# Strassen products in 23 instead of 20 of the down-projection's 44 weight pairs, five of them from sums made earlier

## The chip, the core and the metric

The kernel runs on one core of one Trainium2 chip. The metric is the device time of one launch in microseconds, all loads and stores included. The five engines have queues of their own: TensorE (PE) multiplies, VectorE (DVE) and ScalarE (ACT) work elementwise, GpSimd (POOL) helps with small things, and SyncE (SP) issues nearly all DMA transfers, one after the other in the order of the program.

## What is computed

The reference is one layer of a decoder for 256 tokens of width 2048: a mixing block (sparse attention beside a convolution module), then a gated MLP with a causal depthwise convolution of three taps, then a last RMSNorm. The change lies in the MLP, whose inner width is 5632:

```python
def conv_glu_ffn(h, w_up, cw, cb, w_down):
    u = causal_depthwise_conv(h @ w_up, cw, cb)
    a, gate = jnp.split(u, 2, axis=-1)
    return (jax.nn.silu(gate) * a) @ w_down
...
        h = rms_norm(x, ffn_norm_g[l])
        x = x + conv_glu_ffn(h, w_up[l], ffn_conv_w[l], ffn_conv_b[l], w_down[l])
    return rms_norm(x, final_norm_g)
```

All numbers are float32. The kernel writes each factor as a rounded high part and a low rest (both in the type fp32r) and adds three partial products: high by high, low by high and high by low.

## The kernel before

**Up-projection.** It has 22 groups, m = 0 to 21, and each group uses four weight chunks of 128 x 2048 numbers (1 MB): first the a half of the inner columns, then the gate half, each in two halves of the depth. A group gives 256 inner columns for all 256 tokens. Behind the matmuls a list of stages follows each half group, one stage per chunk: `join` and `three_taps` (bias and convolution), and after the gate half also `gate` (silu times a, the tile g32), `g_high` and `g_low` (the high part stays in the tile gh, the low part goes through the tile glt to DRAM, glf).

**Down-projection.** Its depth of 5632 is cut into 22 pairs of 2 x 128 rows, and its 2048 output columns into two halves, h = 0 and 1, so there are 44 weight pairs of 1 MB, used in the order h = 0, p = 0 to 21, then h = 1. A pair is a 2 x 2 block product: two token halves by two depth tiles by two column blocks of 512. A pair of kind D makes it in the plain way with 8 block products. A pair of kind S uses Strassen's method (Winograd's form) with 7 block products. For that it needs four sums of its weight blocks, made by DVE in `down_split` into the tile `sums` and split into the tiles xh and xl, and four sums of the activation blocks. The latter are made once per p in the up-projection by `g_sums` on POOL, split into gsht and gslt, stored to DRAM (gsf0h, gsf0l, ...) and loaded back as gsh and gsl two pairs ahead by `sum_load`. One block product is four matmuls in `mm_down` (lines 200 to 203): activation block high by weight high (512 columns), low by high (256 columns), high by low (512), low by high (the other 256). With S pairs at p = 4, 6, 8, 9, 11, 13, 14, 16, 18 and 19 in both halves there are 20 of kind S and 24 of kind D.

**Weight stream.** All chunks stand in one list. Three buffers (`wraw`) take the loads. `w_next` hands over the weights of the chunk that is due and calls `w_split` or `down_split` for chunks up to two ahead: ACT writes the high part, DVE the low part, and then `w_dma` emits the next load of the list. That load waits until its buffer, three chunks back, has been read. Every DMA of the stream, the stores of glt, gsht and gslt and the loads of gl (the low activations), gsh and gsl stand in SP's one queue in the order in which the program emits them.

**Where the two stages meet.** In `down_pair` for the first pair the remaining up-projection stages are flushed (with the last two stores of glt), the pool `fu` of the up-projection's working tiles is closed, and the pool `fd` is opened in its memory (`late_pool`: wh4, wl4 for every fourth pair, sums, gsh, gsl). Then come `sum_load`, `w_next` and the products:

```python
            run_todo(3)
            sum_load(22 * h + p + 2)
            ws = w_next()
...
            for name, gi, w in products(kind, j):
```

Of the kernel before, what the change touches and what calls it, by code (L numbers as in the profile page):

```python
# [17 lines left out]
P = 128  # L18
# [20 lines left out]
SPAIRS = (4, 6, 8, 9, 11, 13, 14, 16, 18, 19)  # L39
KINDS = ["".join("DS"[p in SPAIRS] for p in range(22))] * 2  # L40

# [10 lines left out]
def hybrid_trunk(ctx: ExitStack, tc: tile.TileContext, a: dict, out: bass.AP):  # L52
# [20 lines left out]
    for qr, g in OUT_ORDER:  # L73
        chunks.append((a["w_o"][qr, g], CW))
    for m in range(NFT // 2):
        for part in range(2):
            for kh in range(2):
                chunks.append((a["w_u"][m, part, kh], CW))
    for h in range(2):
        for k2 in range(NFT // 2):  # L80
            chunks.append((a["w_d"][h, k2], CW))

    down0 = len(chunks) - NFT
    kinds = {down0 + i: k for i, k in enumerate(KINDS[0] + KINDS[1])}
# [3 lines left out]
    late, lows, late_pool = [], [], []  # L88
# [18 lines left out]

    def down_split(c):

        for f in lows[:]:  # L110
            f()
        lows.clear()
        raw = raws.pop(c)
        if (c - down0) % 4 == 3:
# [5 lines left out]
        if kinds[c] == "D":  # L120
# [7 lines left out]
        b, x = [raw[:, i * 512:(i + 1) * 512] for i in range(4)], late_pool[0].tile([P, CW], F32, name="sums", bufs=1)  # L128
        raw_low = sub_split(h[:, :1536], l[:, :1536], raw[:, :1536])
        nc.vector.tensor_add(x[:, :1024].rearrange("p (a c) -> p a c", a=2),  # L130
                             raw[:, :1024].rearrange("p (a c) -> p a c", a=2), b[3][:, None].to_broadcast([P, 2, 512]))
        nc.vector.tensor_add(x[:, 1024:1536], x[:, :512], b[1])
        nc.vector.tensor_add(x[:, 1536:], x[:, 1024:1536], b[2])  # L133
        raw_low()
        w_dma()
        lows.append(sub_split(xh, xl, x))

    def w_split(cuts):
# [5 lines left out]
        if c in kinds:  # L144
            return down_split(c)
# [23 lines left out]
    def w_next(cuts=1, ahead=LA):  # L169
        c = st["use"]  # L170
        st["use"] += 1
        w_pump()
        if st["split"] >= len(chunks):
            for f in lows:
                f()
            lows.clear()
        while st["split"] <= min(c + ahead, len(chunks) - 1):
# [832 lines left out]
    with ExitStack() as fx:  # L1010
# [3 lines left out]
        fu = up_only.enter_context(tc.tile_pool(name="fu", bufs=2))  # L1014
        gh_all = fp.tile([P, NFT, 2, P], F32R, name="gh")
# [22 lines left out]
        def sum_load(u):  # L1038
            if u < len(PAIRS) and PAIRS[u] == "S":
# [120 lines left out]
        def down_pair(h, p, g, j, nb):  # L1160
# [12 lines left out]
            if kind == "S":  # L1173
# [68 lines left out]
        for h in range(2):  # L1242
            nb = dict(zip((2, 3, 4, 8, 1, 5, 6, 7), ring[4 * h:] + ring[:4 * h]))
            for q in range(NQ):
# [13 lines left out]
                for j in range(2):  # L1258
                    p = 2 * q + j
                    down_pair(h, p, g, j, nb)  # L1260
                    if KINDS[h].rfind("S") == p:
# [92 lines left out]
```

## Time and profile before

| what | value |
|---|---|
| median of 3 runs (range) | 1093.67 us (1093.57 to 1093.92) |
| the profiled execution | 1093.86 us, its span 1092.1 us |
| up-projection, first to last matmul start | 362.5 to 852.3 us |
| down-projection, first to last matmul start | 852.4 to 1083.6 us |
| busy, share of the span | PE 99%, weight loads 88%, DVE 78%, ACT 55%, POOL 19% |
| HBM traffic | 226.29 MB read, 13.13 MB written |

The span runs from the first to the last instruction of the profiled execution, and its own time is 1.8 us longer. Matmuls of 512 columns have durations of about 394 ns in the rows, but follow one another in less, since they overlap, so the pace is read from starts. The releaser in square brackets is what ended the idle time of an engine before an instruction. For a DMA row the time is that of its issue on SP's queue.

### The profile page before, as it was taken

How to read it: one execution, taken by the hardware profiler on the slowest of the kernel's cores; microseconds unless marked ns; L12 is line 12 of the kernel's file. 1: busy time of each engine (PE TensorE's matmuls, PEld its weight loads, DVE VectorE, ACT ScalarE, POOL GpSimd, SP SyncE). 2: the span in 40 equal slices, each digit the busy share in tenths (PEclk: the TensorE clock that was granted, in tenths of full speed). 3: DMA queues.
4: the chain of work that ended last, by engine and by line, in shares of the span. 5: the costliest groups of instructions: out<-in, count | busy, mean ns of one | idle time of the engine just before them, and what ended most of it. 6: DMA issues, size and time to landing. Idle time of an engine off the chain costs nothing.

```text
span 1092.1 us, 17198 instructions
## 1 busy us (share of the span) xinstructions
PE 1080.5 (99%) x6778; PEld 959.7 (88%) x6778; DVE 857.2 (78%) x1369; ACT 601.2 (55%) x873; POOL 204.6 (19%) x171
## 2 busy tenths in 40 slices
PE   9999999999999999999999999999999999999997
PEld 8999999987788888888888888888888888888886
DVE  6899985776456677778777877887777899898996
ACT  7544456778635555555555555555555655554553
POOL 0888856647100000000000000000000000000000
PEclk9999999999999999999999999999999999999998
DMA  9676526323464655656566656665567688858982
GB/s 363 242 264 238 184 92 232 117 79 113 167 229 167 224 189 197 211 200 222 203 223 230 221 198 208 231 213 198 218 228 281 232 310 313 338 223 305 324 306 78
DMA packets 48125, 240.54 MB, mean 220 GB/s; under 512 B 5627, under 2 KB 7947, under 8 KB 24364
## 3 DMA queue, kind: packets, MB, share of 16 engines
q1 hardware_dynamic: 44668, 232.89, 59.9%
q10 hardware_dynamic: 3376, 6.55, 1.7%
q8 instruction: 53, 0.87, 0.3%
q14 instruction: 28, 0.23, 0.1%
HBM read 226.29 MB, written 13.13 MB: 219 GB/s over the span
## 4 chain that ended last, share of the span: by engine, by line
PE 92%; DVE 3%; DMA 3%; ACT 1%; issue 1%; POOL 0%; DVEq 0%; POOLq 0%; ACTq 0%
PE bank L1134 30%; PE bank L1136 15%; PE bank L200 6%; PE bank L202 6%; PE bank L191 5%; PE bank L193 4%; PE bank L192 4%; PE bank L203 3%; PE bank L201 3%; PE bank L210 3%; PE bank L208 3%; PE bank L209 3%; DMA wraw<-in_w_t 1%; PE bank L880 1%; PE bank L860 1%; DVE wl L158 1%
## 5 line engine op out<-in xcount | busy, mean ns | idle before, releaser
L1134 PE MATMUL bank<-xt,wh 128*128 128x512 f32 x1408 | 488.6, 394 | 0.0
L153 ACT ACTIVATE wh<-wraw 128x1024 fp32r<-128x1024 f32 (+2 forms) x193 | 269.9, 1418 | 293.3 <-issue 136.3
L1136 PE MATMUL bank<-xt,wl 128*128 128x256 f32 x1408 | 390.0, 277 | 0.0
L158 DVE TENSOR_TENSOR wl<-wraw,wh 128x2048 fp32r<-128x2048 f32 (+1 forms) x139 | 260.4, 1880 | 113.6 <-ACT wh L153 113.4
L1134 PEld LDWEIGHTS bank<-xt,wh 128*128 128x128 f32 x1408 | 264.0, 188 | 61.3
L1136 PEld LDWEIGHTS bank<-xt,wl 128*128 128x128 f32 x1408 | 264.2, 188 | 0.0
L191 PE MATMUL bank<-xt,wh 128*128 128x256 f32 x512 | 146.7, 287 | 0.9 <-ACT wh L301 0.9
L193 PE MATMUL bank<-xt,wl 128*128 128x256 f32 x512 | 145.2, 284 | 0.1
L192 PE MATMUL bank<-xt,wh 128*128 128x256 f32 x512 | 144.9, 283 | 0.0
L158 POOL TENSOR_TENSOR wl<-wraw,wh 128x1024 fp32r<-128x1024 f32 (+1 forms) x54 | 121.2, 2282 | 31.1 <-ACT wh L153 31.1
L105 ACT ACTIVATE wh<-wraw 128x2048 fp32r<-128x2048 f32 (+1 forms) x44 | 75.5, 1717 | 49.8 <-DMA wraw<-in_w_d 40.4
L191 PEld LDWEIGHTS bank<-xt,wh 128*128 128x128 f32 x512 | 98.0, 191 | 2.6 <-ACT wh L301 1.3
L192 PEld LDWEIGHTS bank<-xt,wh 128*128 128x128 f32 x512 | 98.1, 192 | 0.5
L193 PEld LDWEIGHTS bank<-xt,wl 128*128 128x128 f32 x512 | 98.1, 192 | 0.5 <-DVE wl L158 0.3
L106 DVE TENSOR_TENSOR wl<-wraw,wh 128x2048 fp32r<-128x2048 f32 (+1 forms) x44 | 89.9, 2044 | 7.2 <-ACT wh L105 7.2
L444 DVE SCALAR_TENSOR_TENSOR bank<-us,cw,bank 128x256 f32<-128x256 f32 x232 | 93.8, 481 | 1.0 <-ACT bank L439 0.5
L1047 POOL TENSOR_TENSOR gs<-g 128x256 f32<-128x256 f32 x10 | 7.4, 738 | 437.5 <-DVE g L1086 437.5
L200 PE MATMUL bank<-wh,gh 128*128 128x512 f32 x215 | 84.4, 393 | 0.0
L202 PE MATMUL bank<-wl,gh 128*128 128x512 f32 x215 | 84.4, 393 | 0.0
L1074 DVE SCALAR_TENSOR_TENSOR yt<-u,vecs,yt 128x255 f32<-128x255 f32 (+1 forms) x176 | 81.0, 481 | 3.1
L237 POOL TENSOR_TENSOR rstd<-ms,half 128x1 f32<-128x1 f32 x4 | 2.2, 556 | 346.4 <-DVE ms L230 346.4
L105 ACT ACTIVATE xh<-sums 128x2048 fp32r<-128x2048 f32 x20 | 38.4, 1921 | 49.9 <-DVE sums L133 49.9
(246 smaller groups left out, 1682.8 us busy)
## 6 DMA issues: line engine op xcount, KB each, us to landing
wraw<-in_w_u SPq DMA_DIRECT2D x88, 1024.0 KB, 4.9
wraw<-in_w_d SPq DMA_DIRECT2D x44, 1024.0 KB, 6.8
wraw<-in_w_t SPq DMA_DIRECT2D x29, 1024.0 KB, 5.0
wraw<-in_w_o SPq DMA_DIRECT2D x16, 1024.0 KB, 4.9
gl<-glf SPq DMA_DIRECT2D x22, 512.0 KB, 4.0
glf<-glt SPq DMA_DIRECT2D x22, 256.0 KB, 2.1
wraw<-in_w_vg SPq DMA_DIRECT2D x4, 608.0 KB, 3.7
hb<-in_head SPq DMA_DIRECT2D x4, 512.0 KB, 9.1
```

Source lines behind the costliest of these rows:

```text
L105: nc.scalar.activation(hi, src, AF.Copy)
L106: return lambda: nc.vector.tensor_sub(lo, src, hi.bitcast(F32))
L153: nc.scalar.activation(h[:, sl], raw[:, sl], AF.Copy)
L158: (nc.gpsimd if pooled else nc.vector).tensor_sub(l[:, sl], raw[:, sl], h[:, sl].bitcast(F32))
L191: nc.tensor.matmul(ps, wh, xh, start=first, stop=False)
L192: nc.tensor.matmul(ps, wh, xl, start=False, stop=False)
L193: nc.tensor.matmul(ps, wl, xh, start=False, stop=last)
L200: nc.tensor.matmul(ps, xh, wh, start=first, stop=False)
L202: nc.tensor.matmul(ps, xh, wl, start=False, stop=False)
L444: nc.vector.scalar_tensor_tensor(y[:, j] if last else acc[0], us[:, j, k:k + T], cw[:, j, k:k + 1], acc[0], op0=OP.mult, op1=OP.add)
L1134: nc.tensor.matmul(bk[i], wh[:, k, sl], xt[kt // 4][:, kt % 4].rearrange("p a t -> p (a t)"), start=kt == 0, stop=False)
L1136: nc.tensor.matmul(bk[i][:, :T], wl[:, k, sl], xt_h[kt], start=False, stop=kt == KD - 1)
```

## The change

Three more of the 44 pairs become Strassen pairs: 11 in the first column half and 12 in the second. Five of the 23 are of a new kind P: (h, p) = (0, 2), (0, 11), (1, 2), (1, 4), (1, 12). For these the weight block sums are made during the up-projection. Their weight chunk is put into the list a first time (kind X) ahead of the groups m = 2, 5, 9, 12 and 16. When its turn comes, `early_sums` makes the sums in the tile `early`, and the next `w_next` stores them to DRAM (sumf0 to sumf4). In the down-projection a P pair takes two entries of the list: the weights again, and behind them the sums from DRAM (kind T), which are then split without additions. The set of p that need activation sums is the union over both halves and grows from 10 to 15. Each column half keeps S pairs at p = 18 and 19, so the two stretches of work behind the last Strassen pair of a half stay as they are.

```diff
-SPAIRS = (4, 6, 8, 9, 11, 13, 14, 16, 18, 19)
-KINDS = ["".join("DS"[p in SPAIRS] for p in range(22))] * 2
+KINDS = ("DDPSDSDDSSDPSDDSSDSSDD",
+         "DDPDPSDSSDSDPSDSSDSSDD")
+SPAIRS = [p for p in range(22) if KINDS[0][p] + KINDS[1][p] != "DD"]
+EARLY = [(h, p) for h in range(2) for p in range(22) if KINDS[h][p] == "P"]
...
     for m in range(NFT // 2):
+        for i, (h, p) in enumerate(EARLY):
+            if m == 2 + i * 18 // len(EARLY):
+                kinds[len(chunks)] = "X", sums_far[i]
+                chunks.append((a["w_d"][h, p], CW))
...
             chunks.append((a["w_d"][h, k2], CW))
+            if KINDS[h][k2] == "P":
+                kinds[len(chunks)] = ("T",)
+                chunks.append((sums_far[EARLY.index((h, k2))], CW))
...
+    def block_sums(x, raw):
+        b = [raw[:, i * 512:(i + 1) * 512] for i in range(4)]
+        nc.vector.tensor_add(x[:, :1024].rearrange("p (a c) -> p a c", a=2),
+                             raw[:, :1024].rearrange("p (a c) -> p a c", a=2), b[3][:, None].to_broadcast([P, 2, 512]))
+        nc.vector.tensor_add(x[:, 1024:1536], x[:, :512], b[1])
+        nc.vector.tensor_add(x[:, 1536:], x[:, 1024:1536], b[2])
+
+    def early_sums(c):
+
+        x = up_pool[0].tile([P, CW], F32, name="early", bufs=1)
+        block_sums(x, raws.pop(c))
+        w_dma()
+        stores.append((kinds[c][1], x))
...
+        if kind == "S":
+            x = late_pool[0].tile([P, CW], F32, name="sums", bufs=1)
+            block_sums(x, raw)
+            raw_low()
+            w_dma()
+            lows.append(sub_split(xh, xl, x))
+        else:
+            raw_low()
+            w_dma()
+            st["split"] += 1
+            x_low = sub_split(xh, xl, raws.pop(c + 1))
+            lows.append(lambda: (x_low(), w_dma()))
...
         w_pump()
+        for there, here in stores:
+            nc.sync.dma_start(there, here)
+        stores.clear()
...
-            if u < len(PAIRS) and PAIRS[u] == "S":
+            if u < len(PAIRS) and PAIRS[u] != "D":
                 sq.append([late_pool[0].tile([P, 4, P], F32R, name=n, bufs=2) for n in ("gsh", "gsl")])
```

How the instructions stand, at the places where the prediction counts them. First SP's queue where the up-projection ends, before. The wraw loads are weight pairs in their order: 8376, 8422 and 8473 are pairs 1, 2 and 3 of h = 0, 8554 is pair 4, 8592 pair 5 and 8642 pair 6. The two stores of glt are the last of the up-projection.

```order
L98 DMA wraw_8376<-in_w_d 128x2048
L98 DMA wraw_8422<-in_w_d 128x2048
L98 DMA wraw_8473<-in_w_d 128x2048
L1104 DMA glf10_4140<-glt_8475 128x512
L1104 DMA glf10_4140<-glt_8542 128x512
L98 DMA wraw_8554<-in_w_d 128x2048
L98 DMA wraw_8592<-in_w_d 128x2048
L1035 DMA gl_8626<-glf3_4133 128x1024
L1042 DMA gsh_8628<-gsf0h_4141 128x512
L1042 DMA gsl_8629<-gsf0l_4142 128x512
L98 DMA wraw_8642<-in_w_d 128x2048
```

The same place in SP's queue now (8478 is pair 1, 8524 pair 2, 8575 the sums of pair 2, 8662 pair 3, 8702 pair 4, 8714 pair 5; gsf0 belongs to pair 2, gsf1 to pair 3).

```order
L116 DMA wraw_8478<-in_w_d 128x2048
L116 DMA wraw_8524<-in_w_d 128x2048
L116 DMA wraw_8575<-sumf0_76 128x2048
L1148 DMA glf10_4147<-glt_8577 128x512
L1148 DMA glf10_4147<-glt_8644 128x512
L1086 DMA gsh_8652<-gsf0h_4148 128x512
L1086 DMA gsl_8653<-gsf0l_4149 128x512
L116 DMA wraw_8662<-in_w_d 128x2048
L1086 DMA gsh_8697<-gsf1h_4150 128x512
L1086 DMA gsl_8698<-gsf1l_4151 128x512
L116 DMA wraw_8702<-in_w_d 128x2048
L116 DMA wraw_8714<-in_w_d 128x2048
```

The load of pair 3 stood ahead of the last two stores of glt and stands behind them now, and behind the loads of gsh and gsl of pair 2. Pair 3 was of kind D and is of kind S.

DVE at the same place, before: behind the last low part of the up-projection come pairs 2 and 3 (plain), then pair 4 with its sums.

```order
L106 TENSOR_TENSOR glt_8542<-g32_8537,gh_4125 128x512
L106 TENSOR_TENSOR wl_8551<-wraw_8422,wh_8550 128x2048
L106 TENSOR_TENSOR wl4_8589<-wraw_8473,wh4_8588 128x2048
L130 TENSOR_TENSOR sums_8636<-wraw_8554 128x1024
L132 TENSOR_TENSOR sums_8636<-sums_8636,wraw_8554 128x512
L133 TENSOR_TENSOR sums_8636<-sums_8636,wraw_8554 128x512
L106 TENSOR_TENSOR wl_8633<-wraw_8554,wh_8632 128x1536
L106 TENSOR_TENSOR xl_8635<-sums_8636,xh_8634 128x2048
```

And DVE now:

```order
L124 TENSOR_TENSOR glt_8644<-g32_8639,gh_4132 128x512
L124 TENSOR_TENSOR wl_8657<-wraw_8524,wh_8656 128x1536
L124 TENSOR_TENSOR xl_8659<-wraw_8575,xh_8658 128x2048
L128 TENSOR_TENSOR sums_8709<-wraw_8662 128x1024
L130 TENSOR_TENSOR sums_8709<-sums_8709,wraw_8662 128x512
L131 TENSOR_TENSOR sums_8709<-sums_8709,wraw_8662 128x512
L124 TENSOR_TENSOR wl4_8705<-wraw_8662,wh4_8704 128x1536
L124 TENSOR_TENSOR xl_8707<-sums_8709,xh_8706 128x2048
```

The first sums of the down-projection stand one pair earlier, on pair 3, with the low rest of the stored sums of pair 2 ahead of them.

DVE in the up-projection now, where the first X chunk has its turn: the three additions stand between a chunk's convolution and the low part of the next weights.

```order
L1118 SCALAR_TENSOR_TENSOR yt_4433<-u_4387,vecs_92,yt_4433 128x254
L128 TENSOR_TENSOR early_4469<-wraw_4381 128x1024
L130 TENSOR_TENSOR early_4469<-early_4469,wraw_4381 128x512
L131 TENSOR_TENSOR early_4469<-early_4469,wraw_4381 128x512
L195 TENSOR_TENSOR wl_4476<-wraw_4427,wh_4475 128x2048
```

Nothing of the old work is taken away there; the additions are inserted.

More of the change, by code (lines that the diff above doesn't have):

```diff
@@ L74, in hybrid_trunk @@
         chunks.append((a["w_o"][qr, g], CW))
+    kinds, pair_no = {}, {}
+    far = ctx.enter_context(tc.tile_pool(name="far", bufs=1, space=bass.MemoryType.DRAM))
+    sums_far = [far.tile([P, CW], F32, name=f"sumf{i}") for i in range(len(EARLY))]
     for m in range(NFT // 2):
+        for i, (h, p) in enumerate(EARLY):
+            if m == 2 + i * 18 // len(EARLY):
+                kinds[len(chunks)] = "X", sums_far[i]
+                chunks.append((a["w_d"][h, p], CW))
         for part in range(2):
@@ L80, in hybrid_trunk, with following @@
         for k2 in range(NFT // 2):
+            kinds[len(chunks)], pair_no[len(chunks)] = (KINDS[h][k2],), 22 * h + k2
             chunks.append((a["w_d"][h, k2], CW))
-    down0 = len(chunks) - NFT
-    kinds = {down0 + i: k for i, k in enumerate(KINDS[0] + KINDS[1])}
+            if KINDS[h][k2] == "P":
+                kinds[len(chunks)] = ("T",)
+                chunks.append((sums_far[EARLY.index((h, k2))], CW))
+    def following(c):
+        c += 1
+        while c in kinds and kinds[c][0] in "XT":
+            c += 1
+        return c
     NR, NB, LA = 3, 3, 2
@@ L87, in hybrid_trunk @@
     raws, parts, pieces = {}, {}, []
-    late, lows, late_pool = [], [], []
+    late, lows, late_pool, up_pool, stores = [], [], [], [], []
     clock = {"pe": 0.0, "dve": 0.0}
@@ L113, in down_split @@
         raw = raws.pop(c)
-        if (c - down0) % 4 == 3:
+        kind = kinds[c][0]
+        if pair_no[c] % 4 == 3:
             h = late_pool[0].tile([P, CW], F32R, name="wh4", bufs=1)
@@ L119, in down_split @@
             l = wpool.tile([P, CW], F32R, name="wl", bufs=NB)
-        if kinds[c] == "D":
+        if kind == "D":
             parts[c] = (h, l)
@@ L127, in down_split @@
         parts[c] = (h, l, xh, xl)
-        b, x = [raw[:, i * 512:(i + 1) * 512] for i in range(4)], late_pool[0].tile([P, CW], F32, name="sums", bufs=1)
         raw_low = sub_split(h[:, :1536], l[:, :1536], raw[:, :1536])
[L130 to L136, printed above, removed]
+        if kind == "S":
[10 more added lines that the diff above has]
+            lows.append(lambda: (x_low(), w_dma()))
     def w_split(cuts):
@@ L144, in w_split @@
         if c in kinds:
-            return down_split(c)
+            return early_sums(c) if kinds[c][0] == "X" else down_split(c)
         n = chunks[c][1]
@@ L170, in w_next @@
         c = st["use"]
-        st["use"] += 1
+        st["use"] = following(c)
         w_pump()
+        for there, here in stores:
+            nc.sync.dma_start(there, here)
+        stores.clear()
         if st["split"] >= len(chunks):
@@ L176, in w_next @@
             lows.clear()
-        while st["split"] <= min(c + ahead, len(chunks) - 1):
+        to = c
+        for _ in range(ahead):
+            to = following(to)
+        while st["split"] <= min(to, len(chunks) - 1):
             w_pump()
@@ L1014, in hybrid_trunk @@
         fu = up_only.enter_context(tc.tile_pool(name="fu", bufs=2))
+        up_pool.append(fu)
         gh_all = fp.tile([P, NFT, 2, P], F32R, name="gh")
@@ L1172, in down_pair @@
             ws = w_next()
-            if kind == "S":
+            if kind != "D":
                 gsum = sq.pop(0)
@@ L1260, in hybrid_trunk @@
                     down_pair(h, p, g, j, nb)
-                    if KINDS[h].rfind("S") == p:
+                    if len(KINDS[h].rstrip("D")) - 1 == p:
                         todo.extend(combine(h, nb))
```

## The prediction

> **What bounds the kernel now.** I read the page's busy times first, then the windows of the stages, then the rows of single instructions where the two stages meet.
>
> ```profile
> PE 1080.5 (99%) x6778; PEld 959.7 (88%) x6778; DVE 857.2 (78%) x1369; ACT 601.2 (55%) x873; POOL 204.6 (19%) x171
> ```
>
> ```profile
> core 0: us, PE busy (x) PEld busy (x) DVE busy (x) ACT busy (x) POOL busy (x), PEclk, DMA share, GB/s
> 497.00:542.00 45.00, 45.00 (x261) 39.36 (x260) 35.48 (x50) 24.34 (x32) 1.97 (x3) 1.00 0.62 212
> 852.00:1076.00 224.00, 224.00 (x1276) 195.94 (x1275) 201.03 (x162) 115.38 (x79) 0.00 (x0) 1.00 0.77 282
> ```
>
> PE is busy without a hole in both stages and at full clock. So every matmul taken away shortens the end by its pace, every hole put in lengthens it, and nothing can be won from waits of PE, since there are none. The pace comes from starts, in the rows of the main lines of the up-projection (1134) and the down-projection (200):
>
> ```profile
> L1134 PE MATMUL bank<-xt,wh x1408: 389/395/476, 362.5 to 852.1; 128*128 128x512 f32 x176
> ...
> L200 PE MATMUL bank<-wh,gh x215: 388/392/400, 852.4 to 1079.5; 128*128 128x512 f32 x108
> L200 PE MATMUL bank<-wh,gsh x19: 392/392/403, 875.5 to 1063.4; 128*128 128x512 f32 x19
> ```
>
> The first product starts at 852.4. The first with gsh is the second product of pair 4, so 4 x 8 + 1 = 33 products lie before it: (875.5 - 852.4) / 33 = 0.700 us a product.
>
> **What is removed.** Three pairs go from 8 products to 7: 3 x 0.700 = 2.1 us off PE's path. That is all the change can win, 0.19%; about 0.2% (2.2 us) is what a measurement of this kernel can tell from no change.
>
> **What is added in the up-projection.** Five loads of 1 MB, five times three additions on DVE, five stores of 1 MB; and for five more p, three POOL instructions, a high part on ACT, a low part on DVE and two stores of 256 KB. The prices:
>
> ```profile
> L130 DVE TENSOR_TENSOR sums<-wraw 128x1024 f32<-128x1024 f32 x20 | 24.5, 1223 | 5.7 <-DMA wraw<-in_w_d 5.5
> L132 DVE TENSOR_TENSOR sums<-sums,wraw 128x512 f32<-128x512 f32 x20 | 13.8, 692 | 0.7
> L106 DVE TENSOR_TENSOR gslt<-gs,gsht 128x512 fp32r<-128x512 f32 x10 | 6.8, 684 | 0.0
> ```
>
> A group takes (852.4 - 362.5) / 22 = 22.3 us, and DVE works 35.5 of each 45 us, so 17.6 us in a group. A group with both additions costs it 1.22 + 2 x 0.69 + 0.68 = 3.3 us more: 20.9 of 22.3 us. POOL is idle there. DMA is busy 0.62 of the time at 212 GB/s, 4.7 MB a group; 2.1 MB of an X and 0.5 MB of sums lift that to 7.3 MB, 330 GB/s, less than it moved at the start of the down-projection (401, below). I cost this stage at nothing. The cover is DVE's free 4.7 us a group; were it gone, the five sets of sums would cost up to 13 us.
>
> **What is moved where the stages meet.** This term decides. Pair 2 now takes two entries of the three-buffer stream, so the load of pair 3 slips behind the last two stores of glt, and `sum_load` puts gsh and gsl of pair 2 ahead of it. These two tiles lie in the pool that opens in the up-projection's memory. SP's queue, ACT and DVE before:
>
> ```profile
> 845.72 0.33 SPq L98 DMA_DIRECT2D wraw<-in_w_d  x1
> 853.64 6.10 SPq L1104 DMA_DIRECT2D glf<-glt  x2
> 859.85 3.30 SPq L98 DMA_DIRECT2D wraw<-in_w_d  x2
> ...
> 864.24 0.37 SPq L1042 DMA_DIRECT2D gsh<-gsf0h  x1
> 864.66 0.43 SPq L1042 DMA_DIRECT2D gsl<-gsf0l  x1
> ...
> 875.35 0.43 SPq L1042 DMA_DIRECT2D gsh<-gsf1h  x1
> 875.82 0.43 SPq L1042 DMA_DIRECT2D gsl<-gsf1l  x1
> 876.34 0.38 SPq L98 DMA_DIRECT2D wraw<-in_w_d  x1
> ```
>
> ```profile
> 862.05 1.92 ACT L105 ACTIVATE wh<-wraw 128x2048 fp32r<-128x2048 f32 x1 [1.58 <-DMA glf<-glt]
> 865.11 1.49 ACT L105 ACTIVATE wh<-wraw 128x1536 fp32r<-128x1536 f32 x1 [1.14 <-DMA wraw<-in_w_d]
> ...
> 883.58 1.50 ACT L105 ACTIVATE wh<-wraw 128x1536 fp32r<-128x1536 f32 x1 [1.87 <-DMA wraw<-in_w_d]
> ```
>
> ```profile
> 866.21 1.22 DVE L130 TENSOR_TENSOR sums<-wraw 128x1024 f32<-128x1024 f32 x1
> ...
> 870.87 2.29 DVE L106 TENSOR_TENSOR xl<-sums,xh 128x2048 fp32r<-128x2048 f32 x1 [0.32 <-ACT xh L105]
> ```
>
> The load of pair 3 went out at 845.7. The second store of glt is issued just before 859.8, and the first tile of the new pool (wh4 of pair 3) was free at 862.05, when that store had landed. Now gsh is the first user of that pool, so SP stands until about 862.05. Queued behind it on SP: gsl (issued at about 862.5), pair 3's weights (862.9, each issue some 0.43 us by the rows), gsf1, and the weights of pairs 4 and 5. Who waits: PE for gsl in pair 2's second product, then ACT and DVE, and PE again, for pair 3.
>
> When do pair 3's weights land? Page 6 gives the durations:
>
> ```profile
> wraw<-in_w_u SPq DMA_DIRECT2D x88, 1024.0 KB, 4.9
> wraw<-in_w_d SPq DMA_DIRECT2D x44, 1024.0 KB, 6.8
> gl<-glf SPq DMA_DIRECT2D x22, 512.0 KB, 4.0
> glf<-glt SPq DMA_DIRECT2D x22, 256.0 KB, 2.1
> gsh<-gsf1h SPq DMA_DIRECT2D x2, 256.0 KB, 3.8
> gsl<-gsf1l SPq DMA_DIRECT2D x2, 256.0 KB, 5.1
> ```
>
> From below: alone, as in the up-projection, 862.9 + 4.9 = 867.8. From above: the same queue of gsh, gsl and weights, with a gl in front, was issued from 875.35 (pair 8's weights at 876.34) and ACT could start on the weights at 883.58: 8.2 us after gsh, so 862.05 + 8.2 = 870.3. The gl of 512 KB is not in front here; by 4.9 against 2.1 us for 768 KB less it is worth 1.9 us, which gives 868.4, and loads stand close behind here that share the engines. I take **868.8**.
>
> When does PE want them? Pairs 0 and 1 are plain, pair 2 has 7 products: pair 3 starts at 852.4 + 23 x 0.700 = 868.5, and the third matmul of its fourth product, the first that reads xl, stands 3.5 products later, at 870.95. From the arrival to the end of xl DVE and ACT take what they took for pair 4: 870.87 + 2.29 - 866.21 = 6.95 us, and some 0.1 us of hand-over. So PE gets on at 868.8 + 7.05 = 875.85, **4.9 us late** (3.9 and 6.4 us by the two bounds). The wait for gsl in pair 2 lies inside this: gsh and gsl by their medians land at 865.9 and 867.6, wanted from 864.3, up to 3 us, and what PE loses there it no longer loses at pair 3. Before, pair 3 was plain and had been loaded by 850, and pair 4, the first with sums, had a load issued at 859.85 that landed by 865.1 and a start only at 874.8.
>
> **The rest of the down-projection.** DVE loses 5 sums of 2.6 us and gains three sets of low rests; 201 of 224 us before, about the same now, at nothing. P pairs bring 1 MB more each, three new pairs 0.5 MB of gsh and gsl each. DMA moved here:
>
> ```profile
> 862.00:872.00 10.00, 10.00 (x59) 8.76 (x58) 8.41 (x7) 6.50 (x4) 0.00 (x0) 1.00 1.01 401
> 902.00:912.00 10.00, 10.00 (x60) 8.78 (x59) 9.52 (x8) 5.22 (x3) 0.00 (x0) 1.00 0.96 358
> ```
>
> The densest stretch is h = 1, pairs 2 to 13: three P, five S and four D. Per pair a weight load of 1.05 MB, 0.26 of gl, for S and P 0.52 of gsh and gsl, and for P another 1.05: 3 x 2.88 + 5 x 1.83 + 4 x 1.31 = 23.0 MB. PE needs (8 x 7 + 4 x 8) x 0.700 = 61.6 us for it: 374 GB/s. At 401 it fits, at 358 it takes 64.3 us, 2.7 more. Three buffers carry some of that and PE's late start at pair 3 gives none back here. I take nothing, with 0 to 2.7 us as bounds, more if three buffers aren't enough.
>
> The Trainium skill, "DMA: Bandwidth & Descriptors", section "Specifications", gives about 358 GB/s as the HBM limit of a core. By that rule the 2.7 us would be due (a rival, below); the row of 401 GB/s speaks against it.
>
> **Sum.** 1093.86 of the profiled execution - 2.1 + 4.9 = **1096.7 us**, the span 1092.1 + 2.8 = 1094.9. The median of the runs shown is 0.2 us below the profiled one, which I leave inside the rounding.
>
> **The rivals.**
>
> *The hole slows the clock.* Before, PE runs through, so only the end of the program shows what idle time does, in its last matmul and the windows behind it:
>
> ```profile
> 1083.61 0.28 PE L210 MATMUL bank<-wh,gl 128*128 128x256 f32 x1
> ```
>
> ```profile
> 1084.00:1086.00 2.00, 0.00 (x0) 0.00 (x0) 0.82 (x4) 0.64 (x3) 0.56 (x1) 1.00 0.67 255
> 1086.00:1088.00 2.00, 0.00 (x0) 0.00 (x0) 1.28 (x2) 1.20 (x2) 0.00 (x0) 0.60 0.06 22
> 1088.00:1090.00 2.00, 0.00 (x0) 0.00 (x0) 0.00 (x0) 0.00 (x0) 0.00 (x0) 0.50 0.99 381
> ```
>
> A mean of 0.60 over 1086 to 1088 means half clock from 1086.4 on, 2.5 us after PE's last matmul ended at 1083.9. PE's longest single hole at pair 3, before its first low weights (868.8 + 2.6 + 1.75 = 873.2, less what gsl already cost), is 2 to 4 us. If half clock then lasts as long as the idle time that brought it, 2.5 to 5 us, PE loses 1.3 to 2.5 us: 1098.0 to 1099.2. Against it: the hole is barely long enough. The Trainium skill, "TensorE: Matmul & The Clock Gate", "Part 1: The HAM clock gate (the "warmup" mystery)", has the clock set by free-running windows of about 3.4 us; by that a hole shorter than one falls into it whole or not by chance, and half clock for one or two windows would make 1.7 to 3.4 us.
>
> *DMA becomes the bound* in h = 1, pairs 2 to 13: 2.7 us at 358 GB/s, and twice that if P pairs, which take two of the three buffers, leave the third too late: 1099.4 to 1102. For it, and against it, that ACT waits for weight loads in this stage already, while PE never does:
>
> ```profile
> L105 ACT ACTIVATE wh<-wraw 128x2048 fp32r<-128x2048 f32 (+1 forms) x44 | 75.5, 1717 | 49.8 <-DMA wraw<-in_w_d 40.4
> ```
>
> *Not slower: SP isn't held.* If gsh and gsl fall on memory that was free earlier, pair 3's load goes out at 859.9, as pair 4's did, and lands at 865.1; PE is then 1.2 us late: 1093.0. If even that is hidden, 1091.8. It decides from an arrival before 866.0 on. For it: gsh and gsl were issued at 864.24 without a wait of their own. Against it: 862.05, and that they need memory of the same pool.
>
> *The up-projection doesn't hide the sums*: DVE's low weights come late in groups with X; up to 13 us, 1110. Against it: 4.7 us are free in a group, 3.3 are used.
>
> **Chances.** Forecast 0.50, clock 0.16, DMA 0.15, SP not held 0.15, up-projection 0.04. The forecast's own range by the bounds of the arrival is 1095.7 to 1098.2. For 8 in 10 I cut a tenth on each side, most of the SP case below and the far ends of DMA and up-projection above: 1094.3 to 1101. Faster by over 0.2% is nearly out, since 2.1 us is all there is: 0.03. Within 0.2%: the SP case and the forecast's early end (arrival by 868.0), 0.28. Slower: 0.69.
>
> **What would show it.** In the profile after: PE 12 matmuls fewer and 0.700 us a product as before; SP issuing gsh of pair 2 at about 862.0 and pair 3's weights at 862.9, ACT's high part of pair 3 waiting for DMA until about 868.8, PE's first holes at about 864.5 and 870, together 4.9 us, and none later; the up-projection ending at 852.4 as before. A window with a granted clock below 1.00 around 870 to 880 would show the clock rival, waits of PE after 960 the DMA rival. An end of the up-projection moved by over 0.3 us, or a down-projection without a hole, would make the forecast wrong.

## The result, and the profile after

The changed kernel takes 1103.78 us (median; 1101.99 to 1105.47) where the kernel before takes 1093.65 us on the same chip: a ratio of 1.0091, 95% interval 1.0079 to 1.0103. So it is slower, as forecast, but by 10 us and not by 3, and the time lies above the range. The profiled execution took 1102.44 us with a span of 1100.7 us, 8.6 us longer than that of before (1092.1). Everything below is worked out against these 8.6 us.

First the row of the up-projection's main line, then windows of the up-projection and of the down-projection, the second up to 1084 where that of before ends at 1076. Behind the length stand the busy times of PE, weight loads, DVE, ACT and POOL, then the granted clock, the DMA share and GB/s:

```profile
L1178 PE MATMUL bank<-xt,wh x1408: 389/395/476, 362.3 to 851.9; 128*128 128x512 f32 x176
```

```profile
497.00:542.00 45.00, 45.00 (x262) 39.35 (x261) 36.09 (x50) 24.54 (x32) 1.98 (x3) 1.00 0.64 225
852.00:1084.00 232.00, 227.52 (x1282) 197.84 (x1281) 199.76 (x157) 119.19 (x82) 0.00 (x0) 0.99 0.82 301
```

The up-projection is as long as before (489.6 us from first to last start). In the down-projection PE now has 4.5 us without work, and the granted clock is below 1. Both lie where the stages meet. The two waits of PE in the down-projection that its rows name:

```profile
871.57 0.79 PE L243 MATMUL bank<-wh,gh 128*128 128x512 f32 x1 [2.52 <-ACT wh L123]
874.44 0.80 PE L245 MATMUL bank<-wl,gh 128*128 128x512 f32 x1 [1.87 <-DVE wl L124]
```

The same place on SP's queue, on ACT and on DVE:

```profile
853.45 6.09 SPq L1148 DMA_DIRECT2D glf<-glt  x2
861.40 0.32 SPq L1086 DMA_DIRECT2D gsh<-gsf0h  x1
861.77 0.43 SPq L1086 DMA_DIRECT2D gsl<-gsf0l  x1
862.25 0.42 SPq L116 DMA_DIRECT2D wraw<-in_w_d  x1
862.72 0.43 SPq L1086 DMA_DIRECT2D gsh<-gsf1h  x1
863.19 0.43 SPq L1086 DMA_DIRECT2D gsl<-gsf1l  x1
863.73 1.26 SPq L116 DMA_DIRECT2D wraw<-in_w_d  x2
```

```profile
870.03 1.49 ACT L123 ACTIVATE wh<-wraw 128x1536 fp32r<-128x1536 f32 x1 [8.38 <-DMA wraw<-in_w_d]
```

```profile
870.04 1.22 DVE L128 TENSOR_TENSOR sums<-wraw 128x1024 f32<-128x1024 f32 x1 [6.07 <-DMA wraw<-in_w_d]
...
874.70 2.29 DVE L124 TENSOR_TENSOR xl<-sums,xh 128x2048 fp32r<-128x2048 f32 x1 [0.31 <-ACT xh L123]
```

SP waited with gsh until 861.40, the weights of pair 3 went out at 862.25 and could be used at 870.03. In the windows around it the granted clock is the third number from the right:

```profile
868.00:871.50 3.50, 1.05 (x7) 0.65 (x5) 1.42 (x2) 1.47 (x1) 0.00 (x0) 1.00 1.03 404
871.50:878.40 6.90, 4.96 (x14) 3.88 (x15) 6.56 (x5) 5.10 (x4) 0.00 (x0) 0.51 0.94 380
878.40:882.00 3.60, 3.60 (x23) 3.15 (x22) 3.53 (x5) 0.13 (x1) 0.00 (x0) 1.00 0.92 314
```

By PE's starts pair 2 takes 3.25 us and pair 3 4.42 us more than 7 x 0.700 us: **7.7 us at the join**, the place where the two stages meet. From pair 4 on no pair is late.

The other part is at the end. PE's last product begins 5.6 us later than before (1088.95 for 1083.37), but the span ends 8.6 us later. Behind PE's last work the end takes 11.7 us instead of 8.7: **3.0 us at the end**. The rows of DVE before the change, where its last low rest of the weights and its last sums of results lie:

```profile
1067.52 2.29 DVE L106 TENSOR_TENSOR wl<-wraw,wh 128x2048 fp32r<-128x2048 f32 x1 [0.47 <-ACT wh L105]
1070.53 1.29 DVE L1193 TENSOR_TENSOR x<-bank,x 128x512 f32<-128x512 f32 x2 [0.72 <-PE bank L210]
...
1083.92 0.42 DVE L1222 TENSOR_TENSOR x<-bank,x 128x256 f32<-128x256 f32 x1 [0.36 <-PE bank L210]
```

And after:

```profile
1074.82 4.49 DVE L124 TENSOR_TENSOR wl<-wraw,wh 128x2048 fp32r<-128x2048 f32 x2
1079.22 1.28 DVE L1237 TENSOR_TENSOR x<-bank,x 128x512 f32<-128x512 f32 x2
...
1091.87 0.41 DVE L1266 TENSOR_TENSOR x<-bank,x 128x256 f32<-128x256 f32 x1
```

Before, DVE waits for PE here (0.72, 0.36 and once 0.2 us, 1.3 us in all): PE sets the end. After, DVE waits for PE nowhere: it is itself late, and its work sets the end. I call **lead** the time from the end of DVE's last low rest to the start of PE's last product: before 1083.37 - 1069.81 = 13.6 us, after 1088.95 - 1079.3 = 9.65. With 1.3 us to spare, a lead of 12.3 us is what the end needs.

DVE lost the lead in the second half of the columns. The stretch from the first product of h = 1 to DVE's last low rest, before and after:

```profile
968.10:1069.80 101.70, 101.70 (x583) 89.14 (x582) 90.09 (x67) 53.07 (x37) 0.00 (x0) 1.00 0.78 284
```

```profile
974.90:1079.30 104.40, 104.40 (x594) 91.22 (x593) 90.31 (x66) 55.01 (x40) 0.00 (x0) 1.00 0.85 317
```

Its work is the same, 90.1 and 90.3 us, but it is idle for 14.1 us instead of 11.6, while PE has two products less to do, 1.4 us. The longest of these waits, and SP's queue ahead of it:

```profile
985.85 2.29 DVE L124 TENSOR_TENSOR wl<-wraw,wh 128x2048 fp32r<-128x2048 f32 x1 [7.88 <-ACT wh L123]
```

```profile
975.05 0.33 SPq L1079 DMA_DIRECT2D gl<-glf  x1
975.43 0.43 SPq L1086 DMA_DIRECT2D gsh<-gsf0h  x1
975.91 0.42 SPq L1086 DMA_DIRECT2D gsl<-gsf0l  x1
976.43 0.85 SPq L116 DMA_DIRECT2D wraw<-in_w_d  x2
```

```profile
SPq L1079 <- PE bank L253: 8.2, 1, 8.2
```

Pair (1,2) takes two entries of the stream, so the load of pair (1,3) stands one pair further down SP's queue than a weight load did before, here behind a load of gl that waited 8.2 us for PE to finish with its buffer. Its own buffer had been read by 970.5, but it went out at 976.4, and DVE was idle until 985.85.

### The profile page after: what moved, and what is told of

The parts are those of the page before. It is cut to its first block, busy times and chain, and to the rows that moved or that the text cites. A ratio compares the mean times of both kernels' runs of the same rounds, so it can differ in the third digit from the quotient of the medians.

```text
span 1100.7 us, 17288 instructions
## 1 busy us (share of the span) xinstructions
PE 1081.9 (98%) x6766; PEld 959.6 (87%) x6766; DVE 873.7 (79%) x1386; ACT 608.0 (55%) x881; POOL 213.3 (19%) x186
## 4 chain that ended last, share of the span: by engine, by line
PE 80%; DVE 8%; DMA 5%; ACT 3%; issue 3%; POOL 0%; SPq 0%; DVEq 0%; POOLq 0%; ACTq 0%
PE bank L1178 29%; PE bank L1180 14%; PE bank L234 5%; PE bank L236 4%; PE bank L235 4%; PE bank L245 3%; PE bank L243 3%; PE bank L253 3%; PE bank L251 3%; PE bank L252 3%; DMA wraw<-in_w_d 3%; PE bank L246 1%; DMA wraw<-in_w_t 1%; PE bank L244 1%; DVE wl L124 1%
## 5 line engine op out<-in xcount | busy, mean ns | idle before, releaser
L195 DVE TENSOR_TENSOR wl<-wraw,wh 128x2048 fp32r<-128x2048 f32 (+1 forms) x139 | 261.5, 1888 | 96.0 <-ACT wh L190 95.9
L123 ACT ACTIVATE wh<-wraw 128x1536 fp32r<-128x1536 f32 (+1 forms) x44 | 73.6, 1685 | 45.1 <-DMA wraw<-in_w_d 40.0
L124 DVE TENSOR_TENSOR wl<-wraw,wh 128x1536 fp32r<-128x1536 f32 (+1 forms) x44 | 88.0, 2007 | 12.7 <-ACT wh L123 12.7
L1091 POOL TENSOR_TENSOR gs<-g 128x256 f32<-128x256 f32 x15 | 11.1, 739 | 426.8 <-DVE g L1130 426.8
L243 PE MATMUL bank<-wh,gh 128*128 128x512 f32 x197 | 78.0, 396 | 2.5 <-ACT wh L123 2.5
L245 PE MATMUL bank<-wl,gh 128*128 128x512 f32 x197 | 78.0, 396 | 1.9 <-DVE wl L124 1.9
L123 ACT ACTIVATE xh<-sums 128x2048 fp32r<-128x2048 f32 x18 | 34.5, 1919 | 52.3 <-DVE sums L131 52.3
```

What stands on the lines that cost most here:

```text
L123: nc.scalar.activation(hi, src, AF.Copy)
L124: return lambda: nc.vector.tensor_sub(lo, src, hi.bitcast(F32))
L195: (nc.gpsimd if pooled else nc.vector).tensor_sub(l[:, sl], raw[:, sl], h[:, sl].bitcast(F32))
L243: nc.tensor.matmul(ps, xh, wh, start=first, stop=False)
L245: nc.tensor.matmul(ps, xh, wl, start=False, stop=False)
```

## The experiments

Theory: the second stream entry of a P pair brings the next weight load behind instructions of SP that wait. At the join that costs PE directly, and in the second half it costs DVE, which has little to spare at the end. Rivals: the additions in the up-projection cost something; half clock is what the join costs; three more Strassen pairs ask for more DMA than can be moved, in whatever order.

### The up-projection's additions alone

The kernel before with all of the change's work in the up-projection; its down-projection is left as it was. The edit is shown against the changed kernel, as in all runs but those of the kernel before.

```diff
-KINDS = ("DDPSDSDDSSDPSDDSSDSSDD",
-         "DDPDPSDSSDSDPSDSSDSSDD")
+KINDS = ("DDDDSDSDSSDSDSSDSDSSDD",
+         "DDDDSDSDSSDSDSSDSDSSDD")
-SPAIRS = [p for p in range(22) if KINDS[0][p] + KINDS[1][p] != "DD"]
-EARLY = [(h, p) for h in range(2) for p in range(22) if KINDS[h][p] == "P"]
+SPAIRS = [2, 3, 4, 5, 6, 7, 8, 9, 10, 11, 13, 14, 16, 18, 19]
+EARLY = [(0, 2), (0, 11), (1, 2), (1, 4), (1, 12)]
```

> Before's 20 Strassen pairs, and all that the change adds to the up-projection: the five extra weight loads, their sums and stores (nothing reads them) and the activation sums of five more p. If the up-projection hides this, as forecast: 1093.7 us, within 0.4 of before, and the down-projection starts at 852.2 to 852.5. If part of the measured 10 us comes from the sums made early: 1095 or more, up to 1106 (five times 2.6 us of DVE).

1094.21 us, ratio 1.0002 (0.9993 to 1.0012); the last matmul of the up-projection starts at 851.8. The up-projection hides five sets of sums and five stores of 1 MB.

### One half of the columns at a time

The change's kinds in one half, those of before in the other.

```diff
-         "DDPDPSDSSDSDPSDSSDSSDD")
+         "DDDDSDSDSSDSDSSDSDSSDD")
```

> The change's first column half (11 Strassen pairs, P at 2 and 11) with the second half of before: 21 pairs, one product less than before (-0.7 us). If the wait and the half clock at pairs 2 and 3 are a matter of where the two stages meet alone: the same holes as in the changed kernel, 7.5 to 11 us together, and an end of the program with no delay of DVE: 1100.5 to 1104. If the late DVE at the end comes from what is lost at the start: 3 us more, 1103.5 to 1107, with DVE's last additions behind PE's last matmul.

```diff
-KINDS = ("DDPSDSDDSSDPSDDSSDSSDD",
+KINDS = ("DDDDSDSDSSDSDSSDSDSSDD",
```

> The first column half of before with the change's second half (12 Strassen pairs, P at 2, 4 and 12): 22 pairs, two products less (-1.4 us). No pair of kind P or S before pair 4, so no hole where the stages meet and no half clock. If DVE's delay at the end comes from the second half's own P pairs (DMA too full, DVE kept waiting for weights): + 3 us, 1095.3, and DVE idle for several us at pairs 2 to 4 of the second half. If it was left over from the hole at the start: 1092.3.

The first half alone: 1101.35 us, ratio 1.0067 (1.0052 to 1.0082), 8.5 us lost in pairs 2 and 3, half clock for 6.8 us, the end on time (8.6 us behind PE's last product). The second half alone: 1095.95 us, 1.0020 (1.0011 to 1.0030), no hole of PE, full clock, the end 11.65 us behind. So +7.6 and +2.2, together 9.8 of the 10.1 us: two separate losses. In the second, the wait is there without the join:

```profile
978.88 2.29 DVE L124 TENSOR_TENSOR wl<-wraw,wh 128x2048 fp32r<-128x2048 f32 x1 [6.96 <-ACT wh L123]
```

### The change without the loads of stored sums

```diff
-            if KINDS[h][k2] == "P":
-                kinds[len(chunks)] = ("T",)
-                chunks.append((sums_far[EARLY.index((h, k2))], CW))
...
-            st["split"] += 1
-            x_low = sub_split(xh, xl, raws.pop(c + 1))
-            lows.append(lambda: (x_low(), w_dma()))
+            lows.append(sub_split(xh, xl, raw))
```

> The changed kernel without the loads of the stored sums: in a P pair ACT and DVE split the weights themselves in their place (so those products are not the reference's), with the same instructions on every compute engine. The weight stream then has one entry per pair again. If the second entry is what makes the loads late: pair 3's weights out at about 846, a hole of 1 us at most at pair 2, no idle DVE of several us in the second half: 1092 to 1093. If the loads of gsh and gsl behind the new pool were the cause at the join: the hole stays, 1097 or more.

1094.30 us, ratio 1.0005 (0.9996 to 1.0015), 1.3 us above what was expected: 2.3 us are still lost at the join (waits for gsh and gsl, the longest 1.19 us), full clock, the end 9.2 us behind PE's last product; DVE still waits 3.2 us, at pair (1,4). All products, sums and splits are still made, so the second stream entry accounts for some 9.5 of the 10 us. This run can't tell the entry's place on the queue from its bytes, since 5 MB less are loaded.

### PE kept busy in the holes

Seventeen matmuls with a block of zeros stand in pair 3, ten ahead of its first product and seven within that product, ahead of its first matmul with the low weights.

```diff
+        if zfill:
+            zeros(ps, zfill.pop())
...
+                if (h, p, name) == (0, 3, 2):
+                    zfill.append(7)
+                    zeros(nb[2], 10)
```

> The changed kernel with 17 matmuls by a block of zeros put into PE's two holes of pair 3 (10 before its first product, 7 before that product's first low weights; some 0.2 us each). They add zero to a bank, so the result is the same. If the hole's idle time halves the clock and that costs 3.4 us a time: granted clock 1.00 throughout, 1098 to 1100.5, and all runs alike. If the slow stretch behind the hole has another cause: 1102 to 1105.5 as the changed kernel.

```profile
864.00:872.00 8.00, 7.36 (x38) 5.14 (x36) 1.45 (x3) 1.32 (x1) 0.00 (x0) 1.00 0.99 383
872.00:878.00 6.00, 4.90 (x22) 3.34 (x23) 5.65 (x5) 4.75 (x4) 0.00 (x0) 1.00 0.75 291
```

The clock stays at 1.00, but the time is 1103.73 us, ratio 1.0088 (1.0073 to 1.0103): a miss, since 1098 to 1100.5 was expected. The join costs 6.8 us instead of 7.7 although pair 3's weights landed 0.7 us later, so half clock was worth 0.85 us there as it stands, 1.5 us with the later landing counted. At the end nothing is gained, since DVE, and not PE, sets it (12.0 us behind): its last low rest ends at 1080.7, 1.4 us later than in the change. In this run DVE is so late that PE itself waits for it in the second half, for xl in the pairs (1,16) and (1,19), which take 0.7 and 1.0 us longer; in the change no pair behind the join does.

### The loads of weights moved ahead on SP's queue

In `down_pair` the weights come first, then gl, then gsh and gsl. The first run has the change's second half alone, the second the whole change, the third the whole change with the first half's P pair at p = 3.

```diff
-            if j == 0 and h + p:
-                g_load()
...
-            sum_load(22 * h + p + 2)
             ws = w_next()
+            if j == 0 and h + p:
+                g_load()
+            sum_load(22 * h + p + 2)
```

> The kernel with only the second half changed (22 Strassen pairs), and in every pair w_next ahead of g_load and sum_load, so that on SP's queue the weight loads no longer stand behind loads that wait for PE's end of a pair. The same transfers and the same work. If DVE's delay came from the place of the weights' load on SP (pair 3 of the second half went out at 970.2, as soon as PE had ended a pair, where its buffer had been free before): that load goes out 2 us or more earlier, DVE's idle time of 7 us there shrinks below 3, the end is PE's again: 1092.3 to 1093.0. If it came from too many bytes or too much DVE work: 1095 to 1096.5, as with the old order.

> The changed kernel (23 pairs) with the same reordering. Where the stages meet, pair 3's weights go out at 859.9, ahead of gsh and gsl of pair 2, which still wait until about 862 for the new pool and now land behind 1 MB of weights. By the theory that the place on SP's queue decides both losses: no wait for pair 3, a hole of some 2 us for gsl in pair 2, no delay at the end: 1093.7 - 2.1 + 2.2 = 1093.8, 1093 to 1095, granted clock 1.00 or nearly. If the end stays late: 1096 to 1098.

> As the run before, and the first Strassen pair of the first half at 3 instead of 2 (kinds DDDPSDSDSSDPSDDSSDSSDD, still 11 there and 23 in all), so that gsh and gsl of the first one are wanted at about 870 and not at 864. If nothing else is lost: PE without a hole, 1093.7 - 2.1 = 1091.6, up to 1092.3. If DMA's bytes or DVE's work bound the second half after all: 1093.5 or more.

The second half alone: 1093.03 us, ratio 0.9994 (0.9985 to 1.0003), as expected. The load of pair (1,3) goes out at 963.57 instead of 970.18, DVE no longer waits at that pair (7.0 us with the old order), and the end is 9.1 us behind PE. DVE's longest wait is now 3.8 us, at pair (1,4). Its rows for the two pairs:

```profile
970.93 2.29 DVE L124 TENSOR_TENSOR wl<-wraw,wh 128x2048 fp32r<-128x2048 f32 x1
...
978.79 1.76 DVE L124 TENSOR_TENSOR wl<-wraw,wh 128x1536 fp32r<-128x1536 f32 x1 [3.77 <-ACT wh L123]
```

The whole change: 1097.24 us, 1.0028 (1.0016 to 1.0040); 1093 to 1095 was expected. Pair 3's weights are early now (issued 860.27, landed 865.4), and its 4.4 us are gone but for 0.25. But gsl of pair 2 comes last instead, and PE waits there, with half clock behind it, 3.9 us in all:

```profile
866.96 0.77 PE L243 MATMUL bank<-wh,gsh 128*128 128x512 f32 x1 [2.06 <-DMA gsl<-gsf0l]
```

With P at p = 3: 1098.78 us, 1.0046 (1.0033 to 1.0058), where 1091.6 to 1092.3 was expected. The profiled execution took 1101.26 us; its up-projection began 2.2 us later than in the kernel before, so its times are read within the down-projection alone. Pair 3 is on time, but pair 4 loses 7.2 us, and 6.8 us at half clock follow its wait for gsh. Its gsh and gsl stand behind two loads of weights, the second of which waits for DVE, and land at 881.6 and 882.3:

```profile
867.64 4.97 SPq L116 DMA_DIRECT2D wraw<-in_w_d  x2
872.66 0.42 SPq L1079 DMA_DIRECT2D gl<-glf  x1
873.13 0.42 SPq L1086 DMA_DIRECT2D gsh<-gsf2h  x1
```

So the place on the queue decides, both ways: whatever stands behind a waiting load is late.

### Only the loads of gl moved back

```diff
-            if j == 0 and h + p:
-                g_load()
...
             ws = w_next()
+            if j == 0 and h + p:
+                g_load()
```

> Control: the kernel before with the same move (g_load behind w_next), nothing else. If the order matters only where a stored-sum load has shortened the stream, PE has no wait here with either order and the end is as late as DVE's work makes it: 1093.4 to 1094.0, no difference. If the order is worth something by itself, it would be 1 us or more faster, and the gain of the other kernels would have to be measured against this one.

> The change with that one move alone (g_load behind w_next; the P pair stays at p = 2). Two-part theory: the first two gl loads after the join do not stand ahead of pair 3's weights, so the join costs what it cost (excess 7 to 8.5 us, half clock for one or two windows), and only the end comes in time: last matmul to the end of the span 8.7 to 9.4 us instead of 11.7; 1100 to 1101.5. The rival, that the late end is a consequence of the late join or of the traffic, expects 11.5 us at the end and 1102.4 to 1104.

> The change with the first half's P pair at p = 3 instead of 2 (kinds DDDPSDSDSSDPSDDSSDSSDD, 11 pairs as before) and one move in down_pair: g_load stands behind w_next, sum_load stays ahead of it. Two-part theory: the join costs time because pair 3's weights stand behind the stores of glt, and the end costs time because the load of pair (1,3) stands behind a gl that waits for PE. Here both are gone, and gsh and gsl keep their early place. Expected: pair 3's weights land by 850 as before; gsh and gsl of pair 4 are issued at about 865.6, right behind its weights, not at 873 as in the run with sum_load moved too; at most 0.5 us lost in pair 4 (its low rest of the sums ends within 0.3 us of its need); clock 1.00; last matmul to the end of the span 8.6 to 9.3 us; 1091.6 to 1092.6. The rival, that three more Strassen pairs ask for more DMA than the chip moves in any order, expects a late end or new holes: 1094 to 1097.

> The same order, with the first half's P pairs at p = 4 and 11 (kinds DDDDPSDSSDSPSDDSSDSSDD, 11 pairs, sets of activation sums for 13 p instead of 15): the join is that of the kernel before up to pair 4, whose stored sums are loaded where pair 5's weights were. Two-part theory: no hole at the join (excess below 0.3 us), clock 1.00, end 8.6 to 9.3 us behind the last matmul; 1091.6 to 1092.3. The rival of too much DMA traffic expects holes in pairs 5 to 10, where four S and one P pair lie close together: 1093 to 1096.

In the kernel before the order does nothing that can be told: 1094.08 us, 1.0002 (0.9993 to 1.0011). The other three are misses, the last two by 3 us and more. The change with this order: 1102.26 us, 1.0076 (1.0061 to 1.0092); DVE's wait at pair (1,3) is 2.3 instead of 7.9 us, but a new one of 3.85 us stands at 1042.65, behind the P pair (1,12):

```profile
1031.17 0.38 SPq L1086 DMA_DIRECT2D gsl<-gsf10l  x1
1031.65 4.84 SPq L116 DMA_DIRECT2D wraw<-in_w_d  x3
```

```profile
1040.70 1.92 ACT L123 ACTIVATE wh<-wraw 128x2048 fp32r<-128x2048 f32 x1 [4.22 <-DMA wraw<-in_w_d]
```

Three loads of weights within 4.8 us, behind gsh and gsl, land 9 to 11 us after their issue. So the end stays 11.5 us behind. With P at p = 3 the join costs 1.3 us and the end is 10.6 us behind: 1095.63 us, 1.0020 (1.0010 to 1.0030). With P at p = 4 nothing is lost at the join, but pair 13 of the first half, behind the P pair 11, loses 3.6 us, 1.72 of it a wait for weights and the rest mostly half clock; 1097.31 us, 1.0027 (1.0016 to 1.0039). These rows are of an execution of 1098.16 us, the slowest of six from 1094.9 on:

```profile
909.87 0.38 SPq L1086 DMA_DIRECT2D gsl<-gsf7l  x1
910.30 0.90 SPq L116 DMA_DIRECT2D wraw<-in_w_d  x2
```

```profile
917.86 1.92 ACT L123 ACTIVATE wh<-wraw 128x2048 fp32r<-128x2048 f32 x1 [3.04 <-DMA wraw<-in_w_d]
...
920.38 1.91 ACT L123 ACTIVATE wh<-wraw 128x2048 fp32r<-128x2048 f32 x1 [0.61 <-DMA wraw<-in_w_d]
```

My theory that two misplaced loads are all falls with these: each P pair crowds the loads behind it, and with one of them put right the wait appears at another. The rivals came nearer in all three: 11.5 us at the end and 1102.4 to 1104 us for P at 2, 1094 to 1097 for P at 3, 1093 to 1096 for P at 4.

How near is DMA to a limit, then? In the pairs 2 to 13 of h = 1 (986.1 to 1047.7) the change moves 354 GB/s, with the DMA engines busy for 0.94 of the time. Within that it comes still closer to the 404 GB/s of its best 10 us (995 to 1005):

```profile
980.00:1000.00 20.00, 20.00 (x116) 17.46 (x115) 13.70 (x13) 11.68 (x14) 0.00 (x0) 1.00 0.99 385
```

There is little room. But the sum of the bytes alone doesn't decide: of the two kernels with the second half alone, the one with the weights ahead moves nearly as much in these pairs (345 against 354 GB/s, DMA busy 0.93 in both) and ends 2.9 us earlier. So in these two kernels the order on the queue decided which load was late, while DMA was nearly full. How much of the remaining waits is due to bytes and how much to their crowding behind P pairs stays open.

### DVE's work changed, the loads kept

Is it really DVE that sets the end? In the kernel before, two low rests of the second half are written twice, or left out; in the change's second half alone, two are left out by the same edit, those of the pairs (1,14) and (1,17). Where one is left out, PE reads the high part in its place.

```diff
-            sub_split(h, l, raw)()
+            low = sub_split(h, l, raw)
+            for _ in range(2 if c - down0 in (22 + 15, 22 + 17) else 1):
+                low()
```

> The kernel before, where DVE writes the low rest of the plain pairs (1,15) and (1,17) twice, with the same result: 2 x 2.29 = 4.6 us more for DVE, nothing else. In the kernel before DVE's last low rest of the weights ends 13.6 us ahead of PE's last matmul and the span ends 8.7 us behind it; over the other kernels the end grows about 1 us for each us by which that lead falls below some 12.5. Theory (DVE has about 1 us to spare at the end): lead 9.0, end 11.5 to 12.5 us behind PE's last matmul, 1096.6 to 1097.6. Rival (PE alone sets the end, and the late end of the change has to do with its loads): DVE's busy 78% hides it, 1093.6 to 1094.2.

```diff
+            few = c - down0 in (22 + 15, 22 + 17)
+            parts[c] = (h, h if few else l)
...
+            if not few:
+                low()
```

> The kernel before without the low rests of the plain pairs (1,15) and (1,17) on DVE (PE reads the high part in their place, so these two partial products are not the reference's): 4.6 us less for DVE, every matmul and every load kept. Both theories expect no change here, since PE sets the end: 1093.4 to 1094.0. If it became faster by over 1 us, DVE would have set the end already before the change.

> The change's second half alone (the first half as before), without the low rests of the plain pairs (1,14) and (1,17) on DVE (PE reads the high part in their place, so these two partial products are not the reference's): 4.6 us less for DVE, all loads in their old places, the wait at pair (1,3) still there. Theory (the late end is DVE's lateness): lead of DVE's last low rest 13.5 or more instead of 9.4, end 8.6 to 9.0 instead of 11.65 us behind PE's last matmul, 1092.3 to 1093.3. Rival (the end is late for the loads or the stores, not for DVE): 11.0 to 11.7 us, 1095.5 to 1096.2.

| kernel | lead of DVE, us | end behind PE's last product, us | time, us | ratio (95%) |
|---|---|---|---|---|
| before, 4.6 us less for DVE | 14.3 | 8.7 | 1093.94 | 1.0002 (0.9993 to 1.0011) |
| before | 13.6 | 8.7 | 1093.73 | |
| second half, 4.6 us less for DVE | 13.3 | 9.0 | 1092.88 | 0.9991 (0.9982 to 1.0000) |
| second half, weights ahead | 12.45 | 9.1 | 1093.03 | 0.9994 (0.9985 to 1.0003) |
| before, 4.6 us more for DVE | 10.8 | 9.9 | 1095.43 | 1.0017 (1.0007 to 1.0026) |
| change, weights ahead | 10.8 | 10.0 | 1097.24 | 1.0028 (1.0016 to 1.0040) |
| change | 9.65 | 11.7 | 1103.78 | 1.0091 (1.0079 to 1.0103) |
| second half | 9.4 | 11.65 | 1095.95 | 1.0020 (1.0011 to 1.0030) |

The theory holds in direction in all three. Less work for DVE changes nothing in the kernel before and brings 3.1 us in the change's second half, with every load in its old place and a wait of 7.7 us at pair (1,3). More work makes the kernel before slower by 1.7 us. Its size was off: 3 us or more was expected, but 1.6 us of the added work went into waits that DVE had anyway (idle 10.0 instead of 11.6 us), so the lead fell by 2.8 us and not 4.6. The two kernels with a lead of 10.8 us have nearly the same end (9.9 and 10.0 us), though one has the loads of before and the other those of the change. The runs told of above fit in: leads of 12.0, 11.95, 10.1, 9.3, 9.3 and 9.3 us (weights ahead with P at 3; no loads of stored sums; gl moved back with P at 3, at 4 and at 2; PE kept busy) go with ends of 8.65, 9.2, 10.6, 11.4, 11.5 and 12.0 us. Kernels with nearly the same lead differ by some 0.6 us, so the lead is not all. In the run with more work the rows show the same sign as in the change, no wait for PE behind the last low rests:

```profile
1067.93 4.49 DVE L106 TENSOR_TENSOR wl<-wraw,wh 128x2048 fp32r<-128x2048 f32 x2
1072.34 1.28 DVE L1195 TENSOR_TENSOR x<-bank,x 128x512 f32<-128x512 f32 x2
```

## Why the prediction was right and wrong

**What is removed**: right. PE has 12 matmuls fewer, and from the first product of h = 1 to the last PE takes 113.9 to 114.1 instead of 115.3 us for two products less.

**The up-projection at nothing**: right, by its end (851.9) and by the run that has it alone.

**The join**: the chain up to the sums of pair 3 was right, step by step. SP waited with gsh (861.4, predicted 862.05), pair 3's weights went out right behind (862.25, predicted 862.9), and from their arrival to the end of xl it was 870.03 to 876.99, 6.96 us, predicted 6.95. What PE did there was different. The wait for gsh and gsl in pair 2 came to 0.5 us, of up to 3. And PE did not get on when xl was done: it waited for the high and the low part of pair 3 (2.5 and 1.9 us), then ran at half clock and came to xl at 878.42, 1.4 us after it was there. The size was off in two terms. First the landing: predicted 868.8 within 867.8 to 870.3, measured 869.9, 7.7 us after the issue. I took less than the nearest row of the same queue because no gl stood in front, and overlooked how much was issued right behind: gsh and gsl of pair 3 and two more loads of weights by 865, in windows at 380 to 404 GB/s. With 869.9 in place of 868.8 the prediction's own sum gives 6.0 us instead of 4.9, within its bounds. The run with PE kept busy shows that sum at full clock: landing 870.6, so 6.7 us by the same working, and 6.8 measured; there PE did wait for xl, 0.2 us at 877.71. Second, half clock. The rival did occur, in addition, from 871.5 to 878.4, and is the rest, 1.7 us (rival: 1.3 to 2.5). I had set it beside the forecast at 0.16 because PE's longest single wait seemed barely long enough. The wait was 2.5 us, and it was long enough.

The Trainium skill, "TensorE: Matmul & The Clock Gate", "Part 1: The HAM clock gate (the "warmup" mystery)", puts half clock behind at least one idle window of about 3.4 us. The length of the windows agrees with these traces (stretches at half clock of 3.41 or 6.83 us); that a window has to be idle throughout does not (last section).

**The rest of the down-projection**: this is the step that failed: "DVE loses 5 sums of 2.6 us and gains three sets of low rests; 201 of 224 us before, about the same now, at nothing." DVE's work is indeed the same. But the step asked only whether PE would be held, and named as the sign of trouble "waits of PE after 960". There are none, and still the end is 3.0 us late. DVE is on the chain at the end of the program, with 1.3 us to spare, which the rows behind line 1193 of the kernel before showed (its waits for PE there). From PE's side 1.4 us of the saving in h = 1 used that up at once, and 2.5 us more of waiting for weights came on top: 13.6 to 9.65 us of lead. The wait came from the same slip of a weight load that I followed at the join and nowhere else; the pair (1,2) has it too, behind a gl that waits for PE.

**The rival of DMA as the bound** had its place and part of its mechanism right (two of three buffers taken by P pairs in h = 1), and nearly its rate: 354 GB/s in the pairs 2 to 13, where it counted 374 to be needed. Its path was not what happened: PE lost nothing there, since late loads held ACT and DVE and not PE. It was right that this stage was not free, for which the sum took nothing.

**The sum**: -2.1, 7.7 at the join and 3.0 at the end give 8.6 us, the difference of the two spans. The forecast of 2.8 us lacked 5.8: 1.1 for the landing, 1.7 for half clock and 3.0 for the end. The range had its upper end at the DMA rival's, and no case in which a loss at the join and one behind it add up.

**Still open**: the executions of the changed kernel lie near 1102.2 and near 1105.3 us. The granted clock is 0.994 in the first two and 0.993 and 0.992 in the others, which fits one window more at half clock. But a product takes 1.28 us at half clock (875.25 to 876.53) instead of 0.70, so 3.41 us of it cost PE no more than some 1.6 of these 3 us. Only one of the faster two has a profile, so the cause stays open. No version that makes all products as the reference has them beat the kernel before by more than can be told: the nearest is the second half with the weights ahead (1093.03 us). Against the change as it stands that version is some 10.7 us faster.

## What to carry to other kernels

When an edit gives one step two entries of a shared stream, every later load slips by one step; follow the slip to each place where the issuing queue waits, not only to the first. Ask of an engine that is off the critical path what it has to do behind the last matmul: its lead at the end is a budget, and the rows that show how much it waits for PE there tell its size. Cutting PE's work spends that budget too.

## What the runs showed of the hardware

**Half clock came after a window in which PE was idle for half the time or more.** The records of the clock change on a grid of 3.41 us. I took PE's busy share in each such window from its starts and holes, in nine kernels. Windows at full clock with a share of 0.15, 0.18, 0.18, 0.27, 0.40 and 0.50 were followed by half clock; those with 0.52, 0.61, 0.76, 0.79, 0.80, 0.85 and 0.88 were not. A window already at half clock with a share of 0.44, 0.54 or 0.55 was followed by another, one with 0.90 was not. So a hole of 1.72 us was enough where a window was left with 0.50, and where a hole of 2.5 us fell across two windows, the first kept 0.52 and half clock came only behind the second. In the change the windows from 868.1 and 871.5 have shares of 0.27 and 0.44, hence 6.83 us at half clock.

**A load of 1 MB took longer where more was issued around it.** It took 4.9 us in the up-projection, 7.7 us at the join with 0.5 MB issued just ahead of it and 2.5 MB in the 2.8 us behind it, and 9 to 11 us as one of three behind gsh and gsl.
